# A LoRA kernel on one core: A's load moved between x's first two, B's load on ScalarE's queue, w laid out by GpSimd

## The chip, the core and the metric

The kernel runs on one core of a Trainium2 chip. The metric is the device time of one execution in microseconds (us). Matmuls run on TensorE (PE in the profile), transposes and sums on VectorE (DVE), casts and scaling on ScalarE (ACT), memsets and casts on GpSimd (POOL). SyncE (SP) issues the transfers.

## The reference

```python
# x: 16 x 512 x 768 float32, A: 768 x 16, B: 16 x 768, scale = 0.5
lora = np.matmul(np.matmul(x, A), B)
return (x + scale * lora).astype(np.float32)
```

So 8192 tokens of 768 numbers are read, a correction of rank 16 is added to each, and as many are written.

## The kernel before

The 8192 tokens are 64 tiles of 128. They are loaded in seven parts of 2, 6, 8, 16, 16, 14 and 2 tiles (`PARTS`), straight into one large buffer `x_all`, in which the sums are made in place and from which they are stored. The last part takes the place of the first, which must have been stored by then. Work goes in eight groups of 8 tiles, each of two halves of 4.

The path of a group: its halves are cast to half precision (`narrowed`: half 0 on ScalarE, half 1 on GpSimd), transposed in blocks of 32 x 32 by VectorE (`turned`), multiplied by A on TensorE (`projected`, 24 matmuls into `y_ps`), copied with the scale into a block-diagonal tile `y_bd` by ScalarE (four instructions, the spread), multiplied by B on TensorE (`raised`, for two tiles at a time, into one of two PSUM tiles `lora_ps`), and added to x by VectorE (`summed`, two tiles at a time). Each engine has its own list of work, written out by hand; semaphores with counts order them. TensorE runs `raised` of the group before between the two `projected` of a group, in a hardware loop; its first pass raises zeros. VectorE transposes one half of the next group ahead of each two sums. ScalarE casts half 0 of the next group ahead of the spread of this one.

SP issues all transfers: loads 0 and 1, A, B, loads 2 to 4, then load 5 when `s_y` tells of the first projection, and eight stores. A store waits on `s_sum`, which counts the second `raised` of each group, or on `s_last` at the end. Load 6 waits for the landing of the first store (`s_out0`), and the store of part 2 stands behind it.

Before the first group the weights are laid out. The memset of `a_rows` (GpSimd) comes before A's load into it, a second one before B's load into `b_rows`. VectorE transposes A (L214) and packs it into `w_one` with three strided casts (L221); ScalarE copies `w_one` into the four diagonal blocks of `w_bd` (L201), the weights of the projection. B's rows are cast by ScalarE into `b_half`, spread over the partitions by two matmuls with a selection matrix `pick` (L290), and copied out to `b_mm` (L198), the weights of `raised`. All the small buffers lie in the part of `x_all` that load 5 fills later (`spare`), which is why load 5 waits.

Of the kernel before, what the change touches and what calls it, by code (L numbers as in the profile page):

```python
# [13 lines left out]
PARTS = [2, 6, 8, 16, 16, 14, 2]  # L14
# [6 lines left out]
APART = 8  # L21
# [3 lines left out]
def kernel(  # L25
# [8 lines left out]
    nc = tc.nc  # L34
    fp32 = mybir.dt.float32
    P = 128
    Q = 32
    NQ = P // Q
# [4 lines left out]
    R = A.shape[1]  # L43
    NC = D // 64
# [6 lines left out]
    def sb(name, shape, dtype):  # L51
        return nc.alloc_sbuf_tensor(name, shape, dtype).ap()
# [11 lines left out]
    def lent(n):  # L64
        taken[0] += n
        return spare[:, ds(taken[0] - n, n)]
# [6 lines left out]
    a_t = lent(2 * R * Q).rearrange("p (k r c) -> p k r c", k=2, r=R)  # L73
    w_one = lent(NC * R)[0:Q].bitcast(MM_DT).rearrange("p (c k r) -> p c k r", c=NC, k=2)
    b_rows = lent(D)
    b_half = lent(D // 2).bitcast(MM_DT)
    pick = lent(P // 2).bitcast(MM_DT).rearrange("p (b r) -> p b r", b=NQ)
    w_bd = sb("w_bd", [P, NC, 2, P], MM_DT)
    b_mm = sb("b_mm", [P, D], MM_DT)
    xh = [sb(f"xh{h}", [P, SUB, D], MM_DT) for h in range(2)]  # L80
    y_bd = sb("y_bd", [P, GROUP, P], MM_DT)
    lora = [ps(f"lora_ps{i}", [P, 2, D]) for i in range(2)]
    y_ps = ps("ps_yt", [P, GROUP, Q])

    sems = []

    def sem(name):
        sems.append(nc.alloc_semaphore(name))
        return sems[-1]


    parts = []
# [7 lines left out]
    def memory(t2, i, s, n):  # L100
        S = PARTS[i]
        return t2[ds(parts[i], S * P), :].rearrange("(p s) d -> p s d", s=S)[:, ds(s, n), :]

    def held(i, s, n):
        return tiles(where.index((i, s)), n)

    def tiles(t, n):
        return x_all[:, ds(t % ROOM, n), :]

    s_load = [sem(f"s_load{i}") for i in range(len(PARTS))]  # L110
    s_a, s_b = sem("s_a"), sem("s_b")
    s_ready, s_brows, s_pick, s_zero = sem("s_ready"), sem("s_brows"), sem("s_pick"), sem("s_zero")
    s_w, s_bh, s_bp, s_bm = sem("s_w"), sem("s_bh"), sem("s_bp"), sem("s_bm")
    s_narrow = [sem(f"s_narrow{h}") for h in range(2)]
    s_y, s_spread = sem("s_y"), sem("s_spread")
    s_turned = [sem(f"s_turned{h}") for h in range(2)]
    s_lora = sem("s_lora")

    s_free = [sem(f"s_free{p}") for p in range(PAIRS)]

    s_sum, s_last, s_out0, s_out = sem("s_sum"), sem("s_last"), sem("s_out0"), sem("s_out")

    MMS = 2 * NC
# [7 lines left out]
    def on_sync(e):  # L131
        def load(i):
            ld = (i, 0, PARTS[i])
            e.dma_start(out=held(*ld), in_=memory(x2, *ld)).then_inc(s_load[i], 16)

        load(0)
        load(1)
        e.wait_ge(s_ready, 1)
        e.dma_start(  # L139
            out=a_rows[0 : NC * APART : APART, :], in_=A.rearrange("(c e) r -> c (e r)", e=64)  # L140
        ).then_inc(s_a, 16)
        e.wait_ge(s_brows, 1)
        e.dma_start(out=b_rows[0 : R * APART : APART, :], in_=B).then_inc(s_b, 16)
        for i in range(2, len(PARTS) - 2):
            load(i)

        e.wait_ge(s_y, 1)
        load(len(PARTS) - 2)
        for st in STORES:
            i, s, n = st  # L150
            groups = where.index((i, s + n - 1)) // GROUP + 1
            if groups < NG:

                e.wait_ge(s_sum, groups + 2)
            else:
                e.wait_ge(s_last, 1)
            ins = e.dma_start(out=memory(out2, *st), in_=held(*st))
            ins.then_inc(s_out if i else s_out0, 16)
            if i == 1:
                e.wait_ge(s_out0, 16)  # L160
                load(len(PARTS) - 1)

    def narrowed(e, copy, g, h):
        t = g * GROUP + h * SUB
        for i in dict.fromkeys(where[t + k][0] for k in range(SUB)):
            e.wait_ge(s_load[i], 16)
        if g:
            e.wait_ge(s_y, 2 * g + h - 1)
        n = SUB if (t + SUB - 1) // ROOM == t // ROOM else SUB // 2
        for k in range(0, SUB, n):  # L170
            last = copy(out=xh[h][:, ds(k, n), :], in_=tiles(t + k, n))  # L171
        last.then_inc(s_narrow[h], 1)

    def on_gpsimd(e):
        e.memset(a_rows[0 : NC * APART], 0.0).then_inc(s_ready, 1)  # L175
        e.memset(b_rows, 0.0).then_inc(s_brows, 1)  # L176

        e.sem_inc(s_spread, 1)
        for p, s in enumerate(s_free):
            e.sem_inc(s, 1 if p < 2 else 2)  # L180
        e.memset(pick, 0.0).then_inc(s_pick, 1)
        e.memset(w_bd.rearrange("p c k m -> p (c k m)").bitcast(fp32), 0.0)  # L182
        e.memset(y_bd.rearrange("p s m -> p (s m)").bitcast(fp32), 0.0)  # L183
        e.wait_ge(s_pick, 1)
        e.affine_select(  # L185
            out=pick, in_=pick, compare_op=mybir.AluOpType.not_equal, fill=1.0, base=0,
            pattern=[[0, NQ], [-APART, Q]], channel_multiplier=1,
        ).then_inc(s_zero, 1)
        for g in range(NG):
            narrowed(e, e.tensor_copy, g, 1)  # L190

    def on_scalar(e):
        e.wait_ge(s_zero, 1)
        e.wait_ge(s_b, 16)
        e.copy(out=b_half, in_=b_rows).then_inc(s_bh, 1)  # L195
        narrowed(e, e.copy, 0, 0)
        e.wait_ge(s_bp, 1)
        e.copy(out=b_mm, in_=lora[0][:, 0, :]).then_inc(s_bm, 1)  # L198
        e.wait_ge(s_ready, 3)
        for b in range(NQ):  # L200
            last = e.copy(out=w_bd[ds(b * Q, Q), :, :, ds(b * Q, R)], in_=w_one)  # L201
        last.then_inc(s_w, 1)
        for g in range(NG):
            if g + 1 < NG:
                narrowed(e, e.copy, g + 1, 0)
            e.wait_ge(s_y, 2 * g + 2)
            for b in range(NQ):
                q = ds(b * Q, Q)
                last = e.mul(out=y_bd[q, :, q], in_=y_ps[q, :, :], mul=sc)  # L209
            last.then_inc(s_spread, 1)  # L210

    def on_vector(e):
        e.wait_ge(s_a, 16)
        e.transpose(  # L214
            out=a_t[0 : NC * APART].rearrange("i k r c -> i (k r) c"),
            in_=a_rows[0 : NC * APART].rearrange("c (i k r) -> c (k r) i", k=2, r=R),
        ).then_inc(s_ready, 1)
        e.wait_ge(s_ready, 2)
        EACH = Q // APART
        for b in range(NC // EACH):  # L220
            last = e.tensor_copy(  # L221
                out=w_one[:, ds(b * EACH, EACH), :, :],
                in_=a_t[ds(b * Q, Q)].rearrange("i k r (c n) -> i c k r n", n=APART)[..., 0],
            )
        last.then_inc(s_ready, 1)

        def turned(g, h):
            e.wait_ge(s_narrow[h], g + 1)
            v = xh[h].bitcast(fp32)
            e.transpose(out=v, in_=v).then_inc(s_turned[h], 1)  # L230

        def summed(g, p):
            xs = tiles(g * GROUP + 2 * p, 2)
            e.wait_ge(s_lora, (g + 1) * PAIRS + p + 1)
            ins = e.tensor_tensor(out=xs, in0=xs, in1=lora[p % 2], op=mybir.AluOpType.add)  # L235
            if g + 1 < NG or p + 2 < PAIRS:
                ins.then_inc(s_free[p], 1)
            elif p + 1 == PAIRS:
                ins.then_inc(s_last, 1)

        turned(0, 0)

        e.wait_ge(s_lora, 1)
        turned(0, 1)
        for g in range(NG):
            for h in range(2):
                if g + 1 < NG:
                    turned(g + 1, h)
                summed(g, 2 * h)
                summed(g, 2 * h + 1)  # L250

    def on_tensor(e):
# [15 lines left out]
        def raised(p):  # L268
# [16 lines left out]
                mms[2].then_inc(s_sum, 1)  # L285
            mms[-1].then_inc(s_lora, 1)

        e.wait_ge(s_bh, 1)
        for n0, w in ((0, 512), (512, 256)):
            last = e.matmul(  # L290
                lora[0][:, 0, ds(n0, w)], pick.rearrange("p b r -> p (b r)"),
                b_half[:, ds(n0, w)], start=True, stop=True,
            )
        last.then_inc(s_bp, 1)
        e.wait_ge(s_bm, 1)
        e.wait_ge(s_w, 1)
        with e.Fori(0, NG):
            for h in range(2):
                raised(2 * h)
# [2 lines left out]
        for p in range(PAIRS):  # L302
            raised(p)

    on_sync(nc.sync)
    on_gpsimd(nc.gpsimd)
    on_scalar(nc.scalar)
    on_vector(nc.vector)
    on_tensor(nc.tensor)

    nums = [s.num for s in sems]
    assert nums == list(range(nums[0], nums[0] + len(nums)))

    nc.gpsimd.wait_ge(s_last, 1)
    nc.gpsimd.sem_clear(range(nums[0], s_sum.num))
    nc.gpsimd.wait_ge(s_out, (len(STORES) - 1) * 16)
    nc.gpsimd.sem_clear(range(s_sum.num, s_out.num + 1))
    section.close()


# [33 lines left out]
```

## Time and profile before

| | us |
|---|---|
| runs | 125.11, 125.58, 126.81 (median 125.58) |
| the profiled execution, its own time | 124.85 |
| its span | 122.7 |
| VectorE busy | 83.9 (68%) |
| TensorE busy, matmuls | 56.3 (46%) |
| ScalarE busy | 38.7 (32%) |
| GpSimd busy | 26.2 (21%) |
| DMA queue q1, 50.43 MB | 96.8% of 16 engines over the span |
| first packet of load 0 | 1.98 |
| start of the first sum | 29.39 |
| end of the last sum | 106.24 |
| landing of the last store | 121.8 |

The span is what the page and the trace cover; the execution's own time holds 2.15 us more around it. Times inside the span count from its start. A busy share is an average over the whole span: an engine with a small one can still set the time of a stretch, and one that is idle may be waiting for something that costs nothing.

### The profile page before, as it was taken

To read this page: it belongs to the slowest core of one execution; us is meant where nothing else is said; L and a number is where in the kernel's file an instruction comes from. 1 tells how busy PE (TensorE), PEld (TensorE's weight loads), DVE (VectorE), ACT (ScalarE), POOL (GpSimd) and SP (SyncE) were. 2 spreads that over 40 slices of the span, in tenths; PEclk is the share of its full clock that TensorE was granted. 3 is DMA by queue.
4 is the path that set the end of the run, shared out by engine and by line. 5 is a ranking of instruction groups with operands and counts; after the bars stand their busy time and mean duration, and the time that the engine had idled before them with its cause. 6 is when DMAs were issued, how large, how long until landed. Compare 5 with 4: busy or idle time off the path is not lost.

```text
span 122.7 us, 1317 instructions
## 1 busy us (share of the span) xinstructions
PE 56.3 (46%) x530; PEld 37.1 (30%) x530; DVE 83.9 (68%) x52; ACT 38.7 (32%) x47; POOL 26.2 (21%) x19
## 2 busy tenths in 40 slices
PE   0000206976755764844845775576497545000000
PEld 0000003855343452533614534345354422000000
DVE  0003751418999999999999999999979979600000
ACT  0002992092193534254084072353400310000000
POOL 7503500026017008006204401700530000000000
PEclk9999999999999999999999999998559999655555
DMA  3999998899799699999599999899796996898994
GB/s 88 439 433 403 449 529 385 385 513 465 305 513 481 288 513 449 449 435 435 202 449 413 479 401 553 353 497 465 321 497 272 513 497 272 385 513 385 415 413 198
DMA packets 2216, 50.43 MB, mean 411 GB/s; under 512 B 268, under 2 KB 268, under 8 KB 808
## 3 DMA queue, kind: packets, MB, share of 16 engines
q1 hardware_dynamic: 2216, 50.43, 96.8%
HBM read 25.26 MB, written 25.17 MB: 411 GB/s over the span
## 4 chain that ended last, share of the span: by engine, by line
DVE 54%; PE 12%; DMA 7%; ACT 6%; issue 5%; POOL 1%; SPq 1%; POOLq 0%; ACTq 0%
DVE x_sb L235 38%; DVE xh L230 16%; DMA x_sb<-in_B_dram 7%; PE ps_yt L260 6%; PE lora_ps L277 6%; ACT xh L171 2%; ACT w_bd L201 2%; ACT y_bd L209 1%; POOL x_sb L175 1%; SPq L139 1%; ACT x_sb L195 1%; ACT b_mm L198 1%; ACT L195 0%; POOLq L349 0%; SPq L129 0%
## 5 line engine op out<-in xcount | busy, mean ns | idle before, releaser
L235 DVE TENSOR_TENSOR x_sb<-x_sb,lora_ps 128x1536 f32<-128x1536 f32 x32 | 54.1, 1733 | 2.3 <-PE lora_ps L277 2.3
L277 PE MATMUL lora_ps<-b_mm,y_bd 128*128 128x512 f16 (+1 forms) x144 | 30.3, 348 | 25.5 <-ACT y_bd L209 10.0
L171 POOL CAST xh<-x_sb 128x3072 f16<-128x3072 f32 (+1 forms) x9 | 22.1, 2465 | 63.1 <-PE ps_yt L260 56.6
L230 DVE STREAM_TRANSPOSE xh<-xh 128x1536 f32<-128x1536 f32 x16 | 28.2, 1765 | 8.7 <-ACT xh L171 5.9
L171 ACT CAST xh<-x_sb 128x3072 f16<-128x3072 f32 x8 | 22.0, 2751 | 27.5 <-PE ps_yt L260 22.7
L260 PE MATMUL ps_yt<-xh,w_bd 128*128 128x128 f16 x384 | 26.4, 226 | 8.2 <-DVE xh L230 8.2
L260 PEld LDWEIGHTS ps_yt<-xh,w_bd 128*128 128x128 f16 x384 | 24.4, 100 | 13.5 <-issue 13.1
L277 PEld LDWEIGHTS lora_ps<-b_mm,y_bd 128*128 128x128 f16 x144 | 12.7, 101 | 39.0 <-issue 21.9
L209 ACT ACTIVATE y_bd<-ps_yt 32x256 f16<-32x256 f32 x32 | 12.0, 375 | 20.8 <-PE ps_yt L260 20.5
L214 DVE STREAM_TRANSPOSE x_sb<-x_sb 96x1024 f32<-96x1024 f32 x1 | 1.9, 1933 | 11.2 <-DMA x_sb<-in_A_dram 11.2
L290 PE MATMUL lora_ps<-x_sb 128*128 128x512 f16 (+1 forms) x2 | 0.8, 514 | 13.7 <-ACT x_sb L195 13.7
L195 ACT ACT_TABLE_LOAD x1 | 1.3, 1283 | 11.6 <-DMA x_sb<-in_B_dram 11.6
L290 PEld LDWEIGHTS lora_ps<-x_sb 128*128 128x128 f16 x2 | 0.1, 108 | 13.7 <-ACT x_sb L195 13.7
L201 ACT COPY w_bd<-x_sb 32x384 f16<-32x384 f16 x4 | 2.0, 508 | 0.0
L221 DVE CAST x_sb<-x_sb 32x128 f16<-32x128 f32 x3 | 1.5, 508 | 0.1
L182 POOL MEMSET w_bd<- 128x1536 f32 x1 | 1.4, 1382 | 0.0
L175 POOL MEMSET x_sb<- 96x1024 f32 x1 | 0.9, 948 | 0.5 <-SPq L129 0.5
L195 ACT CAST x_sb<-x_sb 128x768 f16<-128x768 f32 x1 | 0.8, 832 | 0.0
L198 ACT CAST b_mm<-lora_ps 128x768 f16<-128x768 f32 x1 | 0.8, 799 | 0.0
L176 POOL MEMSET x_sb<- 128x768 f32 x1 | 0.7, 736 | 0.0
L183 POOL MEMSET y_bd<- 128x512 f32 x1 | 0.5, 525 | 0.0
L185 POOL TENSOR_SCALAR_AFFINE_SELECT x_sb<-x_sb 128x128 f16<-128x128 f16 x1 | 0.3, 309 | 0.0
(5 smaller groups left out, 0.6 us busy)
## 6 DMA issues: line engine op xcount, KB each, us to landing
x_sb<-in_x_dram SPq DMA_DIRECT2D x2, 6144.0 KB, 36.2
out_dram<-x_sb SPq DMA_DIRECT2D x2, 6144.0 KB, 19.7
out_dram<-x_sb SPq DMA_DIRECT2D x2, 3072.0 KB, 14.4
x_sb<-in_x_dram SPq DMA_DIRECT2D x1, 5376.0 KB, 37.1
out_dram<-x_sb SPq DMA_DIRECT2D x2, 2304.0 KB, 21.4
x_sb<-in_x_dram SPq DMA_DIRECT2D x1, 3072.0 KB, 15.2
x_sb<-in_x_dram SPq DMA_DIRECT2D x1, 2304.0 KB, 9.9
x_sb<-in_x_dram SPq DMA_DIRECT2D x2, 768.0 KB, 5.9
```

The lines of the kernel that those rows point to most:

```text
L171: last = copy(out=xh[h][:, ds(k, n), :], in_=tiles(t + k, n))
L175: e.memset(a_rows[0 : NC * APART], 0.0).then_inc(s_ready, 1)
L195: e.copy(out=b_half, in_=b_rows).then_inc(s_bh, 1)
L198: e.copy(out=b_mm, in_=lora[0][:, 0, :]).then_inc(s_bm, 1)
L201: last = e.copy(out=w_bd[ds(b * Q, Q), :, :, ds(b * Q, R)], in_=w_one)
L209: last = e.mul(out=y_bd[q, :, q], in_=y_ps[q, :, :], mul=sc)
L214: e.transpose(out=a_t[0 : NC * APART].rearrange("i k r c -> i (k r) c"), in_=a_rows[0 : NC * APART].rearrange("c (i k r) -> c (k r) i", k= ...
L221: last = e.tensor_copy(out=w_one[:, ds(b * EACH, EACH), :, :], in_=a_t[ds(b * Q, Q)].rearrange("i k r (c n) -> i c k r n", n=APART)[..., 0],)
L230: e.transpose(out=v, in_=v).then_inc(s_turned[h], 1)
L235: ins = e.tensor_tensor(out=xs, in0=xs, in1=lora[p % 2], op=mybir.AluOpType.add)
L260: mm = e.matmul(y_ps[:, ds(h * SUB, SUB), :], w_bd[:, c, k, :], xv[:, :, c, :, k], start=(m == 0), stop=(m == MMS - 1),)
L277: mms.append(e.matmul(t[:, k, ds(n0, w)], y_bd[:, 2 * p + k, :], b_mm[:, ds(n0, w)], start=True, stop=True,))
```

## The change

A's load is issued between loads 0 and 1, so SP's wait for the memset of `a_rows` now stands ahead of load 1. B's load is issued by ScalarE, as its first instruction, behind a wait for the second memset. The seven copies that lay out w are done by GpSimd, each behind a wait for the one before. ScalarE casts the first half of group 0 behind `b_mm` and no longer ahead of it. VectorE's transpose of the second half of group 0 no longer waits for the first `raised` (`s_lora`). The counts that `s_spread` and `s_free` start from are set by SP and no longer by GpSimd; `s_free[1]` gets its one when SP has seen the first `raised`, ahead of load 5. A wait for a load that the engine has waited for already is left out (`here`). The semaphores come from the Tile framework, which clears them with its own at the end, so two clears on GpSimd go; GpSimd waits for the first store's landing and the others'.

```diff
     def sem(name):
-        sems.append(nc.alloc_semaphore(name))
-        return sems[-1]
+        return tc.alloc_semaphore(name)
 ...
         load(0)
-        load(1)
+
+        e.sem_inc(s_spread, 1)
+        for p, n in ((0, 1), (2, 2), (3, 2)):
+            e.sem_inc(s_free[p], n)
         e.wait_ge(s_ready, 1)
         e.dma_start(
             out=a_rows[0 : NC * APART : APART, :], in_=A.rearrange("(c e) r -> c (e r)", e=64)
         ).then_inc(s_a, 16)
-        e.wait_ge(s_brows, 1)
-        e.dma_start(out=b_rows[0 : R * APART : APART, :], in_=B).then_inc(s_b, 16)
-        for i in range(2, len(PARTS) - 2):
+        for i in range(1, len(PARTS) - 2):
             load(i)
+
+        e.wait_ge(s_lora, 1)
+        e.sem_inc(s_free[1], 1)
 
         e.wait_ge(s_y, 1)
         load(len(PARTS) - 2)
 ...
+    here = set()
+
     def narrowed(e, copy, g, h):
         t = g * GROUP + h * SUB
         for i in dict.fromkeys(where[t + k][0] for k in range(SUB)):
-            e.wait_ge(s_load[i], 16)
+            if (h, i) not in here:
+                here.add((h, i))
+                e.wait_ge(s_load[i], 16)
 ...
     def on_gpsimd(e):
         e.memset(a_rows[0 : NC * APART], 0.0).then_inc(s_ready, 1)
         e.memset(b_rows, 0.0).then_inc(s_brows, 1)
-
-        e.sem_inc(s_spread, 1)
-        for p, s in enumerate(s_free):
-            e.sem_inc(s, 1 if p < 2 else 2)
         e.memset(pick, 0.0).then_inc(s_pick, 1)
 ...
-        ).then_inc(s_zero, 1)
+        ).then_inc(s_pick, 1)
+        e.wait_ge(s_pick, 2)
+        e.wait_ge(s_ready, 3)
+        EACH = Q // APART
+        for b in range(NC // EACH):
+            e.tensor_copy(
+                out=w_one[:, ds(b * EACH, EACH), :, :],
+                in_=a_t[ds(b * Q, Q)].rearrange("i k r (c n) -> i c k r n", n=APART)[..., 0],
+            ).then_inc(s_w, 1)
+            e.wait_ge(s_w, b + 1)
+        for b in range(NQ):
+            e.tensor_copy(
+                out=w_bd[ds(b * Q, Q), :, :, ds(b * Q, R)], in_=w_one
+            ).then_inc(s_w, 1)
+            e.wait_ge(s_w, NC // EACH + b + 1)
         for g in range(NG):
             narrowed(e, e.tensor_copy, g, 1)
 
     def on_scalar(e):
-        e.wait_ge(s_zero, 1)
+        e.wait_ge(s_brows, 1)
+        e.dma_start(out=b_rows[0 : R * APART : APART, :], in_=B).then_inc(s_b, 16)
         e.wait_ge(s_b, 16)
         e.copy(out=b_half, in_=b_rows).then_inc(s_bh, 1)
-        narrowed(e, e.copy, 0, 0)
         e.wait_ge(s_bp, 1)
         e.copy(out=b_mm, in_=lora[0][:, 0, :]).then_inc(s_bm, 1)
-        e.wait_ge(s_ready, 3)
-        for b in range(NQ):
-            last = e.copy(out=w_bd[ds(b * Q, Q), :, :, ds(b * Q, R)], in_=w_one)
-        last.then_inc(s_w, 1)
+        narrowed(e, e.copy, 0, 0)
 ...
     def on_vector(e):
 ...
-        e.wait_ge(s_ready, 2)
-        EACH = Q // APART
-        for b in range(NC // EACH):
-            last = e.tensor_copy(
-                out=w_one[:, ds(b * EACH, EACH), :, :],
-                in_=a_t[ds(b * Q, Q)].rearrange("i k r (c n) -> i c k r n", n=APART)[..., 0],
-            )
-        last.then_inc(s_ready, 1)
 ...
         turned(0, 0)
-
-        e.wait_ge(s_lora, 1)
         turned(0, 1)
 ...
     def on_tensor(e):
 ...
+        e.wait_ge(s_pick, 2)
         e.wait_ge(s_bh, 1)
 ...
-        e.wait_ge(s_w, 1)
+        e.wait_ge(s_w, NC * APART // Q + NQ)
 ...
-    nc.gpsimd.wait_ge(s_last, 1)
-    nc.gpsimd.sem_clear(range(nums[0], s_sum.num))
+    nc.gpsimd.wait_ge(s_out0, 16)
     nc.gpsimd.wait_ge(s_out, (len(STORES) - 1) * 16)
-    nc.gpsimd.sem_clear(range(s_sum.num, s_out.num + 1))
```

More of the change, by code (lines that the diff above doesn't have):

```diff
@@ L83 @@
     y_ps = ps("ps_yt", [P, GROUP, Q])
-    sems = []
     def sem(name):
-        sems.append(nc.alloc_semaphore(name))
-        return sems[-1]
+        return tc.alloc_semaphore(name)
     parts = []
@@ L111 @@
     s_a, s_b = sem("s_a"), sem("s_b")
-    s_ready, s_brows, s_pick, s_zero = sem("s_ready"), sem("s_brows"), sem("s_pick"), sem("s_zero")
+    s_ready, s_brows, s_pick = sem("s_ready"), sem("s_brows"), sem("s_pick")
     s_w, s_bh, s_bp, s_bm = sem("s_w"), sem("s_bh"), sem("s_bp"), sem("s_bm")
@@ L176, in on_gpsimd @@
         e.memset(b_rows, 0.0).then_inc(s_brows, 1)
-        e.sem_inc(s_spread, 1)
-        for p, s in enumerate(s_free):
-            e.sem_inc(s, 1 if p < 2 else 2)
         e.memset(pick, 0.0).then_inc(s_pick, 1)
         e.memset(w_bd.rearrange("p c k m -> p (c k m)").bitcast(fp32), 0.0)
-        e.memset(y_bd.rearrange("p s m -> p (s m)").bitcast(fp32), 0.0)
+        e.memset(y_bd.rearrange("p s m -> p (s m)").bitcast(fp32), 0.0).then_inc(s_ready, 1)
         e.wait_ge(s_pick, 1)
@@ L309 @@
     on_tensor(nc.tensor)
-    nums = [s.num for s in sems]
-    assert nums == list(range(nums[0], nums[0] + len(nums)))
-    nc.gpsimd.wait_ge(s_last, 1)
-    nc.gpsimd.sem_clear(range(nums[0], s_sum.num))
+    nc.gpsimd.wait_ge(s_out0, 16)
     nc.gpsimd.wait_ge(s_out, (len(STORES) - 1) * 16)
-    nc.gpsimd.sem_clear(range(s_sum.num, s_out.num + 1))
     section.close()
```

## The prediction

> **What bounds the kernel now.** I read the page first: its slices, its queues and its chain.
>
> ```profile
> span 122.7 us, 1317 instructions
> ...
> DVE  0003751418999999999999999999979979600000
> ...
> DMA  3999998899799699999599999899796996898994
> ...
> q1 hardware_dynamic: 2216, 50.43, 96.8%
> HBM read 25.26 MB, written 25.17 MB: 411 GB/s over the span
> ...
> DVE 54%; PE 12%; DMA 7%; ACT 6%; issue 5%; POOL 1%; SPq 1%; POOLq 0%; ACTq 0%
> ```
>
> The chain names VectorE, and VectorE is full from slice 10 to slice 29. But its shares add up to 86%: the chain stops with the last sum at 106.24 us, and the last 16.4 us of the span are not in it. In those slices all engines are idle and the DMA row is full. One queue carries every transfer, at 96.8% of 16 engines over the span, the empty first 2 us included. Asked one issue at a time, the landings follow the order of issue: loads 0 to 5 at 5.4, 11.3, 18.7, 33.2, 47.8 and 61.3 us, then the stores, the last at 121.8. A store issued at 39.12 lands at 63.2, behind a load issued at 24.19. So the queue always has work, and the end is the start of the queue (2 us) plus 50.43 MB at its rate. 6.29 MB take 14.5 us (load 4, 33.2 to 47.8), which is 432 GB/s, so all bytes need 116.6 us.
>
> The compute matters only where the queue would run dry, that is where a store is issued later than the queue could use it. I compared each store's issue with the landing of the transfer ahead of it. The slack is 8.8 us for the store issued at 69.05, 7.2 us for 99.91 and 8.2 us for 106.26. Only the one issued at 91.02 is tight: what is ahead lands at 92.36. The windows there count packets by their start, and a packet of that size takes 1.8 us:
>
> ```profile
> 88.90:89.50 0.60, 0.60 (x3) 0.29 (x2) 0.46 (x1) 0.00 (x0) 0.60 (x1) 0.50 2.27 983
> 89.50:90.00 0.50, 0.50 (x3) 0.21 (x2) 0.00 (x0) 0.00 (x0) 0.50 (x1) 0.50 0.46 197
> 90.00:90.20 0.20, 0.20 (x2) 0.08 (x1) 0.02 (x1) 0.00 (x0) 0.07 (x1) 0.50 1.13 492
> 90.20:91.80 1.60, 1.60 (x11) 1.02 (x10) 1.60 (x1) 0.00 (x0) 0.00 (x0) 0.56 0.00 0
> 91.80:92.20 0.40, 0.40 (x10) 0.40 (x8) 0.40 (x2) 0.00 (x0) 0.00 (x0) 1.00 4.63 1966
> ```
>
> The last two columns are the DMA share and GB/s. Twelve packets start at 88.9 to 89.5 and end near 91.0; nothing starts until 91.8; then 16 start at once. So 12 DMA engines stand idle for about 0.8 us. But four are behind: two of them start a packet as late as 90.0 to 90.2 and are busy until 91.8 to 92.0. These slowest engines lose only 0.1 us, and the last of the 16 ends the kernel. So even this gap is worth about 0.1 us at the end.
>
> **The change part by part.** The rows for the start:
>
> ```profile
> 0.95 0.95 POOL L175 MEMSET x_sb<- 96x1024 f32 x1 [0.51 <-SPq L129]
> ...
> 1.93 0.90 SPq L139 DMA_DIRECT2D x_sb<-in_A_dram  x1
> ...
> 2.88 0.55 SPq L143 DMA_DIRECT2D x_sb<-in_B_dram  x1
> ...
> 11.56 1.28 ACT L195 ACT_TABLE_LOAD   x1 [11.56 <-DMA x_sb<-in_B_dram]
> ...
> 13.18 1.55 DVE L221 CAST x_sb<-x_sb 32x128 f16<-32x128 f32 x3
> ...
> 17.06 2.07 ACT L201 COPY w_bd<-x_sb 32x384 f16<-32x384 f16 x4
> ...
> 33.26 2.75 ACT L171 CAST xh<-x_sb 128x3072 f16<-128x3072 f32 x1 [4.82 <-DMA x_sb<-in_x_dram]
> ```
>
> *A ahead of load 1.* SP now waits for the memset of a_rows (ends 1.90) ahead of load 1 and all later loads. A's issue stands at 1.93 to 2.83 as before, so load 1 is issued at 2.88 instead of 1.42. Load 0's first packet started 1.0 us after its issue (0.97, 1.98), so load 1's are there at 3.9. Load 0's packets end between 4.1 and 5.0, which covers it by 0.2 us; without that cover each 0.1 us is 0.1 us at the end. The four semaphore increments now on SP (17 ns each, 78 ns apart on GpSimd's queue, 0.3 us) end before 1.9 and are hidden by the same memset. I take 0, bounds 0 to +0.4.
>
> *Arrival of A.* It lands behind load 0, at about 5.7 instead of 11.2; no later than 11.2 in any case. Its VectorE transpose (1.93) then ends at 7.7.
>
> *B from ScalarE's queue.* The issue waits for the second memset (2.58). No row shows two queues. B lands with load 0 at best (5.4) and as before at worst (11.5). The table load (1.28) goes under the flight. Then cast 0.83, two matmuls 0.82, cast 0.80: b_mm is ready at 7.9, or 14.0 at worst. Behind it on ScalarE stands the narrowing of group 0, which needs load 1 (11.3, or 11.4 with A and B ahead of it): it ends at 14.2, or 16.8.
>
> *w on GpSimd.* Seven copies leave VectorE (3 x 508 ns = 1.5 us) and ScalarE (4 x 508 ns = 2.0 us). No row has them on GpSimd. Its casts of 3072 and 1536 elements take 2749 and 1470 ns, so 0.83 ns an element and 0.19 us fixed: 3 x 0.30 + 4 x 0.51 = 2.9 us, plus 0.1 us for each of seven waits on itself, 3.6 in all. With the 508 ns of the other engines it is 4.3. From 7.7 w_bd is ready at 11.3 to 12.0, where it was 19.13. GpSimd's own narrowing of group 0, behind it, starts at 11.4 to 12.0 instead of 11.32.
>
> *First sum.* Narrowing to 14.2, transpose 1.7, projection 2.2, two raises 1.5 to 2.7, projection 1.5 to 2.5, spread 1.5, raise 0.85: the first sum starts at 23.5 to 26, with B late at 28.5, where it was 29.39. The removed wait of VectorE's second transpose for s_lora is inside this.
>
> *Where that lead goes.* The last row above: in the kernel before, ScalarE had already waited 4.8 us for load 3, until 33.26, and load 3 comes no earlier. ScalarE's order puts the spread of group 1 behind that narrowing: it ends 36.0, spread to 37.6, raise to 38.5. The first sum of group 1 then starts at 38.5 instead of 39.40. So of 3 to 6 us of lead, 0.9 us is left, whatever happened before. From there VectorE is full, so the tight store is issued at 90.1 instead of 91.02. The 0.8 us gap goes, worth 0.1 at the end. Loads gated by it (5, on s_y and now s_lora; 6, on the first store) stand in a full queue and cover the rest.
>
> *The tail.* Two clears of semaphores go (183 ns at 106.27, hidden; 47 ns behind the last landing); the last clear now covers 37 instead of 6. Durations of 47, 67 and 183 ns for 4, 6 and 28 semaphores give about 0.23 us for 37: +0.17 - 0.09 = +0.08.
>
> Sum: 124.85 (122.7 and 2.15 around it) + 0 - 0.1 + 0.08 = 124.8 for the profiled execution. That one is 0.73 below the median of the runs shown (125.58). If these runs differ by how late the tight store was, the lead of 0.9 takes most of it back; if by other things, none. I take half: **125.2**.
>
> **The rivals.**
>
> *1. The runs' scatter is the tight store* (124.3). Runs before go from 125.11 to 126.81, so lateness may well reach 2 us, and 0.9 is taken off each. For: the granted clock fell to 0.5 from 84.8 to 91.6, in the group ahead of that store, and cost VectorE 0.81 us there. Against: the slowest DMA engines forgive the first part of it.
>
> *2. TensorE's clock takes the place of the wait.* With the lead, TensorE now idles from about 32 to 37.7, 5 us, while ScalarE waits for load 3. If its clock falls there for one stretch of 6.8 us, as at 84.8, the two raises take 2.7 instead of 1.5 and a projection 2.5 instead of 1.5; the sums of group 1 start 0.5 us later and the next spread is late as well. The lead of 0.9 is gone and the tight store is where it was or 0.2 later: 124.85 + 0.2 + 0.1 = 125.15, by the median 125.8. For: the clock fell 1.5 us after the last matmul (105.3). Against: it also fell at 84.8 with no gap over 1.7 us behind it, so idling alone does not set it. The Trainium skill (TensorE: Matmul & The Clock Gate, "Part 1: The HAM clock gate") says that one idle window of about 3.4 us throttles; by it this rival would be the rule here, since 5 us hold such a window about every second time, and the fall at 84.8 does not agree with it.
>
> *3. Slower: GpSimd's seven copies become the start of everything.* Before, w_bd at 19.13 gave the first sum at 29.39, 10.3 us later. The lead is gone when w_bd comes after 19.1, which takes 1.6 us a copy, and beyond that each us is a us of dry queue at the tight store. At 2.2 us a copy w_bd is ready at 23.1, the store 4 us late: 128.9, by the median 129.6. For: the copies read with a stride, into 32 partitions, and each waits for the one before. Against: it is over four times the 508 ns of either other engine, and GpSimd equals ScalarE on the narrowing (2749 and 2751 ns).
>
> *4. The change doesn't do what it says:* B still lands behind load 1. That is the bound of 28.5 above; the wait for load 3 hides it: 125.3.
>
> **How the numbers follow.** The forecast (with 4, whose time is the same) 0.58, rival 1 0.14, rival 2 0.20, rival 3 0.05, and 0.03 for a gain beyond what I can name: faster by over 2% is under 123.07, that is a span under 120.9, while bytes (116.6), the first 2 us, and 0.35 + 0.9 us from last packet to end make 119.85; so 1.8 of the 2.8 us of all slack would have to go. 2%, about what a measurement of this kernel can tell from no change, is 2.5 us. Faster 0.03, same 0.91, slower 0.06 (rival 3 and a little for loads that start late). The range takes in rivals 1 and 2 with the start's 0.4: 124.2 to 126.5.
>
> **What would show it.** Right: A and B landing by 6 us, w_bd by 12, the first sum at 23 to 26; then ScalarE idle some 8 us for load 3 until 33.3, the sums of group 1 at 38.5; the tight store near 90.1 and no empty window behind it; last landing still at 121.4 to 122. Wrong: loads that land later than before by over 0.4 us, a GpSimd copy over 1.6 us, an empty DMA window anywhere else, or a last landing before 121.

## The result and the profile after

The changed kernel takes 126.75 us (median of six runs, 126.41 to 127.22), the kernel before 125.34 us beside it. The ratio is 1.0124 with a 95% interval of 1.009 to 1.0158. So it is slower by 1.2%, less than 2% but clear of the scatter, and outside the range given (124.2 to 126.5). Here and below a ratio leaves out single runs over 1.5% above the fastest of their kernel, so it can differ a little from that of the medians. The profiled execution took 127.08 us with a span of 125.3, where before it was 124.85 and 122.7.

The page of the changed kernel, the lines that answer to those shown of before:

```profile
span 125.3 us, 1313 instructions
...
DVE  0060082469915999999999999889999979500000
...
DMA  2999999799989989999799999999969959899980
...
q1 hardware_dynamic: 2184, 50.38, 95.0%
q10 hardware_dynamic: 32, 0.05, 0.2%
HBM read 25.26 MB, written 25.17 MB: 403 GB/s over the span
...
DVE 51%; PE 14%; DMA 8%; issue 8%; ACT 3%; POOL 1%; SPq 1%; POOLq 0%; ACTq 0%
```

The bytes are the same, at 403 GB/s instead of 411. B's 0.05 MB went through ScalarE's queue q10. VectorE is full from slice 13 instead of slice 10. The row that matters is DMA: it looks as full as before until the last slices.

The timeline of the start, in the same order as the lines of before:

```profile
1.92 0.87 SPq L138 DMA_DIRECT2D x_sb<-in_A_dram  x1
2.60 0.58 ACTq L208 DMA_DIRECT2D x_sb<-in_B_dram  x1
...
8.31 1.29 POOL L193 CAST x_sb<-x_sb 32x128 f16<-32x128 f32 x3 [3.47 <-DVE x_sb L225]
...
9.66 2.18 POOL L199 COPY w_bd<-x_sb 32x384 f16<-32x384 f16 x4
...
13.37 2.75 ACT L175 CAST xh<-x_sb 128x3072 f16<-128x3072 f32 x1 [2.60 <-DMA x_sb<-in_x_dram]
...
35.12 2.75 ACT L175 CAST xh<-x_sb 128x3072 f16<-128x3072 f32 x1 [9.60 <-DMA x_sb<-in_x_dram]
```

The weights are ready as early as meant: w_bd at 11.84 instead of 19.13. But the first cast of x starts at 13.37 instead of 11.32 (GpSimd's, before), and that of group 2 at 35.12 instead of 33.26. The chain of work says whom they wait for. In the kernel before, its first long piece was B's load; here it is load 1:

```profile
2.85 10.44 DMA x_sb<-in_x_dram
13.29 0.02 issue
13.31 0.02 ACTq L170
13.33 0.04 issue
13.37 2.76 ACT xh L175
```

Load 1 is issued at 2.85 and lands at 13.29, 2.0 us later than before (11.27). A load's semaphore gets one increment from each of the 16 DMA engines, and the trace has their times: 14 of the 16 are in by 11.74, the last two come at 13.01 and 13.29. Every later landing of the queue keeps that tail: load 3 33.53 and then 34.83 and 35.09; the last store 122.43 for the thirteenth, then 123.79, 123.93 and 124.00 (before: all by 121.76). From load 5 on a third is late (62.00, where the thirteenth is in by 61.34). The windows show both ends of it. The columns after the stretch and its length are TensorE's clock, the DMA share and GB/s; first before, then after:

```profile
4.00:5.00 1.00, 1.00 1.18 473
5.00:6.00 1.00, 1.00 1.19 498
6.00:7.00 1.00, 1.00 0.75 313
4.00:9.00 5.00, 1.00 1.03 434
```

```profile
4.00:5.00 1.00, 1.00 1.52 409
5.00:6.00 1.00, 1.00 0.63 261
6.00:7.00 1.00, 1.00 0.92 356
4.00:9.00 5.00, 1.00 1.00 367
...
121.40:122.40 1.00, 0.50 0.56 227
122.40:123.60 1.20, 0.50 0.16 67
```

From 4 to 9 us the queues start 367 GB/s worth of packets instead of 434. That is 0.34 MB less, 0.8 us on the average of 16 engines, but some engines lose 2 us and others little. And from 122.4 on, where the kernel before had ended, the share of 0.16 is 2.6 engines of 16: three late ones finish alone. Two engines start their first packet of load 1 only at 6.51 and 6.71, when the last packet of load 0 on any engine has ended at 5.06. And first packets of load 1 are slow, not only on these two (1.30 and 1.44 us): the longest, 1.72 us, starts at 4.52, where before they take 0.69 to 0.87.

Of the 2.58 us by which the two spans differ, 2.24 are the last landing (124.00 against 121.76) and 0.34 the part behind it (1.27 against 0.93 us).

### The profile page after: what moved, and what is told of

Same layout as the page of the kernel before. It is cut to its first block, busy times and chain, and to the rows that moved or that the text cites. A ratio compares the mean times of both kernels' runs of the same rounds, so it can differ in the third digit from the quotient of the medians.

```text
span 125.3 us, 1313 instructions
## 1 busy us (share of the span) xinstructions
PE 62.0 (50%) x530; PEld 42.2 (34%) x530; DVE 82.5 (66%) x49; ACT 36.9 (29%) x43; POOL 29.3 (23%) x26
## 4 chain that ended last, share of the span: by engine, by line
DVE 51%; PE 14%; DMA 8%; issue 8%; ACT 3%; POOL 1%; SPq 1%; POOLq 0%; ACTq 0%
DVE x_sb L238 35%; DVE xh L233 16%; PE ps_yt L261 9%; DMA x_sb<-in_x_dram 8%; PE lora_ps L278 5%; ACT xh L175 2%; ACT y_bd L220 1%; POOL x_sb L179 1%; SPq L138 1%; POOLq L346 0%; ACTq L170 0%; SPq L125 0%
## 5 line engine op out<-in xcount | busy, mean ns | idle before, releaser
L278 PE MATMUL lora_ps<-b_mm,y_bd 128*128 128x512 f16 (+1 forms) x144 | 32.6, 371 | 25.4 <-issue 8.5
L261 PE MATMUL ps_yt<-xh,w_bd 128*128 128x128 f16 x384 | 30.5, 245 | 9.0 <-DVE xh L233 9.0
L261 PEld LDWEIGHTS ps_yt<-xh,w_bd 128*128 128x128 f16 x384 | 28.2, 110 | 14.1 <-issue 13.5
L278 PEld LDWEIGHTS lora_ps<-b_mm,y_bd 128*128 128x128 f16 x144 | 14.0, 109 | 39.7 <-issue 24.6
L199 POOL COPY w_bd<-x_sb 32x384 f16<-32x384 f16 x4 | 2.0, 500 | 0.2
L193 POOL CAST x_sb<-x_sb 32x128 f16<-32x128 f32 x3 | 1.2, 387 | 3.6 <-DVE x_sb L225 3.5
```

Of the source, the lines that this page charges most:

```text
L199: e.tensor_copy(out=w_bd[ds(b * Q, Q), :, :, ds(b * Q, R)], in_=w_one).then_inc(s_w, 1)
L261: mm = e.matmul(y_ps[:, ds(h * SUB, SUB), :], w_bd[:, c, k, :], xv[:, :, c, :, k], start=(m == 0), stop=(m == MMS - 1),)
L278: mms.append(e.matmul(t[:, k, ds(n0, w)], y_bd[:, 2 * p + k, :], b_mm[:, ds(n0, w)], start=True, stop=True,))
```

## The experiments

In all of them each kernel ran in five rounds beside the kernel before. T1, T2, T3 and T5 are the theories named in the expectations. T1: load 1, issued 1.4 us later, leaves DMA engines without packets, and the slowest sets the end. T2: B's packets on a second queue hold engines up. T3: the compute behind load 3 makes the tight store late. T5, added after the first four: any issue while the engines already run costs, however late it is.

**Load 1 first again, B still on ScalarE's queue.**

```diff
         load(0)
+        load(1)
 ...
-        for i in range(1, len(PARTS) - 2):
+        for i in range(2, len(PARTS) - 2):
             load(i)
```

> The changed kernel with load 1 issued right behind load 0 again, ahead of SP's wait and of A; B stays on ScalarE's queue. Theory T1 (load 1 is issued 1.4 us later, at 2.85 instead of 1.42, so the DMA engines run out of packets at 4 to 5 us, the slowest fall 2 us behind, and a queue that is always full never gives that back): load 1's last landing goes from 13.3 to about 11.4 us, the last store's from 124.0 to under 122.3, time 125.6 to 125.9. Theory T2 (the 16 packets of B on a second queue hold up some engines): load 1 still lands near 13, time 126.7. Theory T3 (the compute behind load 3 makes the tight store late): the first landings don't matter, time 126.7.

Measured: 124.90 us (before 125.11), ratio 0.9969 (0.9938 to 1.0). Load 1's last landing is at 11.43, the last store's at 121.93. T1 holds; T2 and T3 do not, and it came out 0.7 us better than T1 gave.

**B back on SP, A still in between.**

```diff
-        for i in range(1, len(PARTS) - 2):
+        load(1)
+        e.wait_ge(s_brows, 1)
+        e.dma_start(out=b_rows[0 : R * APART : APART, :], in_=B).then_inc(s_b, 16)
+        for i in range(2, len(PARTS) - 2):
             load(i)
```

> The changed kernel with B's load back on SP, behind load 1; A stays between loads 0 and 1. T1: load 1 still lands at about 13, time 126.7. T2: load 1 lands by 11.5, time 125.6. T3: b_mm is ready only at 14, TensorE's work starts later, but ScalarE still waits for load 3; time 126.7.

Measured: 127.21 us, ratio 1.0126 (1.007 to 1.0182). Load 1 lands at 13.54. The loss is there without the second queue, and in the run above the second queue is there without the loss.

**Both back.** The order loads 0, 1, A, B on SP, all else as changed.

> The changed kernel with the four first transfers in the order and on the queue of the kernel before (loads 0, 1, A, B on SP); GpSimd's copies, the shorter programs and the framework's semaphores stay. T1 and T2: load 1 lands at 11.3, time 125.6, that is the kernel before plus the 0.33 us by which the part behind the last landing grew (0.93 to 1.26 us). T3: w on GpSimd comes later still, at about 17, time 126.7 or more.

Measured: 125.10 us, ratio 0.9978 (0.9941 to 1.0014). Load 1 lands at 11.18, the last store at 121.62. GpSimd's w, the shorter programs and the framework's semaphores together change nothing that this tells apart.

**Load 1 late, with A and B behind it.**

```diff
         e.wait_ge(s_ready, 1)
+        e.wait_ge(s_brows, 1)
+        load(1)
         e.dma_start(
             out=a_rows[0 : NC * APART : APART, :], in_=A.rearrange("(c e) r -> c (e r)", e=64)
         ).then_inc(s_a, 16)
```

> As the one with both back, but SP waits for the two memsets ahead of load 1, which so is issued at about 2.6 us, with A and B behind it on SP. T1: the slowest engines fall behind without A in between and without a second queue; load 1 lands at 12.5 to 13.3, time 126.3 to 126.7. T2: load 1 lands as with both back, time 125.6.

Measured: 127.36 us, ratio 1.0153 (1.0098 to 1.0208). Load 1, issued at 2.66, lands at 13.98; 14 engines are in by 12.03. So neither A's packets in front nor the second queue is needed: the late issue alone does it. It came out above what T1 gave and a little above the change itself, whose interval overlaps with this one; its profile has a late tight store as well (issued at 93.00, see the rivals below).

**Load 1 at 1.93 us, and at 4.95 us.** SP waits ahead of load 1 for the first memset only, and for the selection matrix too. Both edits are shown against the run just above; in the first the wait for `s_brows` goes behind A, ahead of B.

```diff
         e.wait_ge(s_ready, 1)
-        e.wait_ge(s_brows, 1)
         load(1)
```

```diff
         e.wait_ge(s_brows, 1)
+        e.wait_ge(s_pick, 2)
         load(1)
```

> As the kernel with late load 1, but SP waits only for the first memset ahead of load 1, so load 1 is issued at about 1.95 us instead of 2.66 (1.41 with both back); A and B behind it on SP. T1 (the engines run out of packets between 4.1 and 5.0 us, and a fresh start takes up to 2.4 us from issue to full speed on the slowest engine: load 0's issue at 0.97, its slowest first packet done at 3.4): 1.95 + 2.4 = 4.35, so at most a few tenths are lost; load 1's last landing 11.2 to 11.8, time 125.1 to 125.6. T5 (any issue while the engines already run costs the same, however late): load 1's last landing 13 to 14, time 127.3.

> As the kernel with late load 1, but SP also waits for the selection matrix on GpSimd (done at 4.85) ahead of load 1, which is so issued at 4.9. T1: every 0.1 us later is 0.1 us lost on all engines now: load 1's last landing 15 to 16, time 128.8 to 129.8. T5: as at 2.66, last landing 14, time 127.4.

Measured: 126.75 us, ratio 1.0107 (1.0074 to 1.0139), for 1.93; 127.82 us, ratio 1.0202 (1.0147 to 1.0257), for 4.95. Both miss what T1 gave, one above and one below it. At 1.93 one engine alone is late: 15 are in by 11.29, the last comes at 12.80. It has no packet from about 4.3 to 5.47 (the profile does not name a packet's engine; this is strung together from the times) and takes 1.70 us for its first, and the last store waits for it until 124.25. T1 had put the cover at 2.4 us from the issue, the end of load 0's slowest first packet; 1.93 + 2.4 = 4.33 should have lost some tenths at most, so that measure is too short. At 4.95 all are late, in by 14.07. The windows of that run, with columns as above, show a stretch in which no engine starts a packet:

```profile
4.00:5.00 1.00, 1.00 0.34 135
5.10:5.90 0.80, 1.00 0.00 0
4.00:9.00 5.00, 1.00 0.72 241
```

The slowest engine lands load 1 at 13.98 when it is issued at 2.66 and at 14.07 when it is issued at 4.95. So "every 0.1 us later is 0.1 us lost" is false. What the issue times show, with one profile each, is a step: the slowest engine lands load 1 1.5 us later than before when it is issued at 1.93, 2.0 at 2.85, 2.7 at 2.66 and 2.8 at 4.95, and being later first adds engines (1, 2 or 3, all) rather than time. T5 is not right either, as the following run shows.

**Load 0 of four tiles**, in the changed kernel.

```diff
-PARTS = [2, 6, 8, 16, 16, 14, 2]
+PARTS = [4, 4, 8, 16, 16, 14, 2]
 ...
-        (0, 0, 2), (1, 0, 6), (2, 0, 8), (3, 0, 16), (4, 0, 16), (5, 0, 8), (5, 8, 6), (6, 0, 2)
+        (0, 0, 4), (1, 0, 4), (2, 0, 8), (3, 0, 16), (4, 0, 16), (5, 0, 8), (5, 8, 6), (6, 0, 2)
```

> The changed kernel, A between the first two loads and B on ScalarE's queue, with parts of 4 and 4 tiles instead of 2 and 6, so that load 0's packets last 1.8 us longer. T1: load 1, issued at 2.85 as before, comes in time; the last of load 1 lands at about 11.4 and not 13.3, time 125.2 to 125.6. T5, and T2 (the second queue): nothing changes, 126.7.

Measured: 125.09 us, ratio 0.9989 (0.995 to 1.0029). Load 1 is issued at 2.85 as in the changed kernel, with A in front and B on the second queue, and now lands at 11.32. The loss is gone by cover alone. This run also has everything the change was to bring: A lands at 7.71, the first sum starts at 23.79, the tight store is issued at 88.72 and no engine runs dry behind it. It takes as long as the one with both back. The early weights are worth nothing in the median.

**The kernel's own semaphores**, on top of load 1 first. The allocation and the two clears are as in the kernel before.

```diff
-        return tc.alloc_semaphore(name)
+        sems.append(nc.alloc_semaphore(name))
+        return sems[-1]
 ...
-    nc.gpsimd.wait_ge(s_out0, 16)
+    nc.gpsimd.wait_ge(s_last, 1)
+    nc.gpsimd.sem_clear(range(nums[0], s_sum.num))
     nc.gpsimd.wait_ge(s_out, (len(STORES) - 1) * 16)
+    nc.gpsimd.sem_clear(range(s_sum.num, s_out.num + 1))
```

> The kernel with load 1 first (A behind it, B on ScalarE's queue), with the semaphores allocated and cleared by the kernel itself as before. The part behind the last landing should go from 1.26 back to 0.93 us, and the time from 124.9 to about 124.55, below the kernel before (125.1 to 125.3). If the framework's semaphores cost nothing, 124.9.

Measured: 124.68 us (before 125.15), ratio 0.9946 (0.9917 to 0.9975). The part behind the last landing is 0.91 us. The median is 0.22 below that of load 1 first, a little less than the 0.36 in the profiles (1.27 to 0.91). This one beats both kernels, the one before by 0.5%. Against that one its profile shows no gain: the span is 122.9, where before it was 122.7. What it gains lies around the span, 1.8 us (median over its runs) instead of 2.2 for the kernel before; nothing on record shows why.

**The kernel before with A alone moved.**

```diff
         load(0)
-        load(1)
         e.wait_ge(s_ready, 1)
         e.dma_start(
             out=a_rows[0 : NC * APART : APART, :], in_=A.rearrange("(c e) r -> c (e r)", e=64)
         ).then_inc(s_a, 16)
+        load(1)
```

> The kernel before with one thing changed: A is issued between loads 0 and 1, so load 1 is issued at about 2.85 us; B follows it on SP, w stays on VectorE and ScalarE, the semaphores are the kernel's own. T1 (an engine that runs out of packets at 4 to 5 us starts again 1 to 2 us late, and the slowest engine ends the kernel): load 1's last landing at 12.8 to 14, the last store's 1.5 to 2.3 us later than before, time 126.4 to 127.2. If the loss needs another part of the change too, 125.2.

Measured: 127.27 us, ratio 1.0141 (1.0103 to 1.0179). Load 1 lands at 13.69, the last store at 124.30. This one move does all of the loss, in a kernel whose tight store is on time (90.90). Its window, beside that of the kernel with both back:

```profile
4.00:9.00 5.00, 1.00 0.98 340
```

```profile
4.00:9.00 5.00, 1.00 1.03 435
```

The DMA share is nearly the same, since a slow packet counts as busy. GB/s tells.

**Load 1 behind the four increments** on SP, all else as with both back.

```diff
         load(0)
-        load(1)
 
         e.sem_inc(s_spread, 1)
         for p, n in ((0, 1), (2, 2), (3, 2)):
             e.sem_inc(s_free[p], n)
+        load(1)
```

> As the kernel with both back, but load 1 stands behind the four semaphore increments on SP, so that it is issued at about 1.7 us, between 1.41 (125.1, nothing lost) and 1.93 (126.75, one engine 1.5 us late). T1 with a step: an engine either has its next packets in time or pays a restart of 1.2 us and more; so 125.1 in most runs, or 126 and over where one engine misses. T1 without a step: 125.2 to 125.6 in all.

Measured: 125.13 us, ratio 1.0 (0.9972 to 1.0027). Load 1, issued at 1.66, lands at 11.29. Nine of twelve runs lie between 124.91 and 125.29, the others are 125.74, 126.19 and 127.09. Together with 1.93 this is the step: between 0.69 and 0.96 us behind load 0's issue. The single long runs would fit an engine that misses now and then, but no profile was taken of one, and the kernel before has such runs too (126.11 to 126.9 in 4 of the 23 beside these).

**Parts of four and four on the best one.** The edit of `PARTS` and `STORES` above, on the kernel with its own semaphores.

> The kernel with load 1 first and its own semaphores (124.68), with parts of 4 and 4 tiles instead of 2 and 6, so that the cover of load 0 is 1.8 us longer. If some engines still lose tenths at the first change of loads (its slowest engine lands load 1 at 11.44, the others by 10.9), 124.2 to 124.5; if not, 124.7.

Measured: 124.66 us, ratio 0.9954 (0.9926 to 0.9983), against 124.68 without. No more is lost at the first change of loads once load 1 is issued right behind load 0.

## Why the prediction was right or wrong

*The bound: right for the median.* The queue is full, the end is its last engine, and compute that is early by some us does not show: the first sum starts at 23.79 in one kernel and at 27.68 in another with the same time (125.09, 125.10). A tight store that comes late does show; that is taken up with the gap and with rival 1 below.

*A ahead of load 1: the term that failed.* It was put at 0, with bounds of 0 to +0.4. It is +1.8 us by the ratio of the one-move kernel (1.0141), 2.1 by the medians (127.27 against 125.16), and came with the sign of being wrong that the text named, loads that land over 0.4 us later. The step in the text was "Load 0's first packet started 1.0 us after its issue", from which load 1's packets were to be there at 3.9, ahead of 4.1. That is the fastest of 16 engines. In the same trace the first packets of load 0 start between 1.98 and 2.90, and the slowest of them ends at 3.41, 2.4 us after its issue. With 2.85 + 2.4 = 5.25 there is no cover (and 2.4 is still too little, as the run at 1.93 shows). Two more things in that step were wrong. The price of a miss is not its length but a restart: two engines in the changed kernel started again only at 6.51 and 6.71, and first packets took up to 1.72 us instead of 0.69 to 0.87. And the text itself had said that the last of the 16 ends the kernel, and then used the first of them.

*The gap at the tight store: it went the other way.* It was to vanish, worth 0.1 us. Load 3 now landed 1.9 us later, and the clock was down from 31.9 on, so the sums of group 1 started at 41.00 and the store was issued at 91.83. In the windows of the changed kernel the gap is there again, for 13 engines:

```profile
90.00:91.00 1.00, 1.00 0.57 246
91.00:92.10 1.10, 1.00 0.01 0
92.10:92.60 0.50, 1.00 0.47 197
92.60:92.80 0.20, 1.00 8.09 3441
```

The three late engines had packets of the store ahead until 94.1 to 94.5 and lost nothing: the slow engines forgive the gap, as the prediction read it in the trace of before. The 13 others lost by it: the store is issued 0.81 us later than before, and they end at 122.27 to 122.43, 0.8 later than the first 14 before (121.48 to 121.63). Behind the three late ones this costs nothing; without them, by these times, it would have set the end.

*The weights: right.* w_bd at 11.84 (11.3 to 12.0 was said); GpSimd's copies take 387 and 500 ns, where 300 and 510 were worked out, and each wait 0.06 us, where 0.1 was taken from no row. A landed at 6.25 (5.7), B at 8.15 (between 5.4 and 11.5), the first sum at 26.46 (23.5 to 26), this one with load 1 two us late.

*The tail: mis-sized.* +0.08 was said and +0.34 came. The clear of 37 semaphores was right (243 ns, 0.23 us said). The rest is what replaced the two clears: behind the last landing GpSimd now runs a wait and a branch before it reports the end (0.24 us from landing to report, 0.11 before), and a drain takes 104 ns instead of 64. Another term pays it back: the 2.15 us around the span, which the sum took over unchanged, are 1.82 in the changed kernel (about 1.8 in all six runs). So the profiled execution is longer by 2.24 + 0.34 - 0.33 = 2.25 us (2.23 measured).

*The rivals.* TensorE's clock fell in the changed kernel at 31.9 us, for 13.7 us, and the lead was gone, as rival 2 had it, but not for its reason: it fell ahead of the wait for load 3 (34.3 to 39.5 without a matmul). Over the other runs the wait does count: in the six where it left TensorE idle for 3.6 to 7.0 us the clock fell within it or at most 0.7 us behind its end, in the three with 3.0 to 3.2 us (load 1 first, both back, own semaphores) it did not. That is where the Trainium skill (TensorE: Matmul & The Clock Gate, "Part 1: The HAM clock gate") puts it, at an idle window of about 3.4 us; but the falls at 84.8 in the kernel before and at 31.9 here, and more in the other runs, have no such gap ahead of them. The price was put on the tight store, and there it is nothing: the run with four tiles first has a fall (at 35.0), the run with both back has none in that wait, and both take 125.1. Rivals 3 and 4 did not come. A small loss at the start was named only as "loads that start late" in the last share of the chances; it should have been a rival with a price.

Rival 1, the scatter, stays open, and the record speaks for its mechanism. With late load 1 the tight store is issued at 93.00, and 14 engines wait for it:

```profile
92.50:93.50 1.00, 1.00 0.00 0
93.80:94.00 0.20, 1.00 8.09 3441
```

There 15 engines end at 123.46 to 123.77, all later than the last one of the kernel before (121.76); the first end is 30.5 us behind the store's issue in both. So a tight store later than 91.02 reads as time at the end, and the early weights keep off that edge (88.5 to 90.3 where load 1 lands in time). The kernel before took over 126 us in 16 of its 81 runs on record, the six kernels with early weights that lose nothing at load 1 in 3 of 72. No long run of the kernel before was profiled, so that these are late tight stores is not shown.

## What to carry to other kernels

Where one full queue sets the time, the end is that of the slowest DMA engine, and an average (share, GB/s, integral of idle time) hides the loss: read the increments of a load's semaphore one by one. Here the last two came 1.3 and 1.6 us behind the others at load 1, and still did at load 4, 36 us on. Keep the first transfers right behind each other and put no wait between them; what is to be fetched early goes behind enough large transfers, or the first one is made long enough to cover the wait. Cover is measured on the slowest engine's first packet at least; at 1.93 us even that was too little.

## What the runs showed of the hardware

- In the changed kernel engines that had run out by 5.06 us started load 1 as late as 6.51 and 6.71. First packets of load 1 took up to 1.72 us (2.28 with load 1 issued at 4.95) instead of 0.69 to 0.87. When load 1 followed load 0's issue by 0.45 or 0.69 us no engine was late, by 0.96 us one was, by 1.7 to 1.9 us two or three, and by 4.0 us all.
- What the slowest engine has lost at 5 us stays until the end of the kernel, 120 us on: 2.0 us at load 1, 2.2 at the last store.
- The time of an execution around its span is 2.2 us in the kernel before, 1.8 in the changed one and 1.9 with both back (medians over their runs). Why was not tried.
- A clear of a range of semaphores took 47, 67, 183 and 243 ns for 4, 6, 28 and 37 of them, about 6 ns each.
- Why the restart takes so long, and why only some engines miss when all get their packets from one issue, was not tried.
